# A transformer kernel whose modulation rows are summed by fused multiply-adds on VectorE

## The chip, the cores and the metric

The kernel runs as one program on 1 core of a Trainium2 chip. The time is the device time of one execution in microseconds. Before the change it was measured three times: 1494.89 us median, 1494.23 to 1496.46. The engines are TensorE (PE, with its weight loads as PEld), VectorE (DVE), ScalarE (ACT), GpSimd (POOL) and SyncE (SP), which here only issues transfers.

## The reference

Three transformer layers run one after the other on one sequence of 256 tokens of width 1024: a first block (sliding-window and differential attention, cross attention, an MLP of 4096) and two layers of a second block, each with two gated feed-forwards of 2816 and an attention part between them. All of it is float32. What the change touches is the modulation of the second block. Each of its two layers turns the vector `c` into nine rows of 1024 that shift, scale and gate the layer:

```
c_act = silu(c)                                   # 1024
for l in range(2):
    mod = c_act @ ada_w[l] + ada_b[l]             # 1024 x 9216 weights
    sh1, sc1, g1, sh2, sc2, g2, sh3, sc3, g3 = split(mod, 9)
    h = rms_norm(x, norm_g[l, 0]) * (1 + sc1) + sh1
    x = x + 0.5 * g1 * swiglu(h, ff_w13[l, 0], ff_w2[l, 0])
    h = rms_norm(x, norm_g[l, 1]) * (1 + sc2) + sh2
    x = x + g2 * (hybrid_conv_mla if l == 0 else nsa_attention)(h)
    h = rms_norm(x, norm_g[l, 2]) * (1 + sc3) + sh3
    x = x + 0.5 * g3 * swiglu(h, ff_w13[l, 1], ff_w2[l, 1])
```

The two modulation matrices are 75.5 MB of weights for a product with one vector.

## The kernel before, in words

**The weight stream.** All weights come from HBM in units of 128 x 2048 float32 (1 MB). `issue` (L383) puts their transfers on SP's queue in one fixed order, each into one of four `raw` buffers, as soon as a buffer is free. A matrix product in float32 accuracy is made of three: a unit is cut in two halves of 1024 columns, and of each half ACT makes a rounded part `whi` and DVE the remainder `wlo` (`pump`, L402, with the subtraction at L415). The activations are split in the same way (`hhi`/`hlo`, `gh`/`gl`, ...). TensorE then takes eight 128x128 tiles of a half and issues three matmuls of 256 columns for each, 24 a half. `pump` keeps the splits three halves ahead of TensorE.

**The order of the work.** The program is a list of steps (`Step`, L241). A step with weights is one half unit: pump, then what earlier steps have deferred, then its matmuls and, at the end of a pair of output tiles, the operations that take the result out of PSUM (`ft`, `x`, `q`, `k` and so on). Each engine takes its own instructions in the order in which the list emits them. In the feed-forwards and the MLP these steps follow each other; in the attention parts they are mixed with small steps of scores, softmax (`nm`, `p`, `r`), transposes (`pT`) and values (`o`).

**The modulation.** `ada_steps` (L716) cuts each matrix in nine sections of 1024 outputs and each section in four units `(s, q)` of two input blocks `k` of 128. A unit is a `raw` step: its 2048 columns are two rows of 1024 per partition, and `self.sc[:, k]` holds silu(c) for block `k`, one number per partition. The sum over the eight blocks is kept in a tile `adacc` of 128 x 1024. The unit is worked off in four pieces of 512 columns (`piece`). For `k == 0` ACT writes raw x sc into `adacc`. For the other seven blocks ACT scales the piece in place (`raw<-raw,sc`) and POOL adds it to `adacc` (L737). With the fourth piece the `raw` buffer is given back. When two sections are done, `rows` sums `adacc` over the partitions on TensorE (`ada<-adacc,Z`, eight matmuls of 512 columns), and `post` transposes the rows into the column tile `M` (`adat`), adding the bias on DVE.

`with_ada` (L783) spreads the 72 units over the steps from the 24th on to the 90th before the last that are not marked quiet. `ADA_LAGS` says how many such steps after the unit's place each of its parts is emitted: the four pieces 0, 0, 1 and 1 steps later, `rows` 3 and `post` 4 steps later.

Of the kernel before, what the change touches and what calls it, by code (L numbers as in the profile page):

```python
# [21 lines left out]
OP = mybir.AluOpType  # L22
# [4 lines left out]
D = 1024  # L27
# [8 lines left out]
LEAD = 1  # L36
HY = 14
NS = 20
ADA_DVE = ()
ADA_LAGS = (0, 0, 1, 1, 3, 4)  # L40
ADA_GAP = 2
GP = 64
NFILL = (0, 1, 4, 5, 10, 13)
# [249 lines left out]
class Kernel:  # L293
# [420 lines left out]
    def ada_steps(self, l):  # L714

        nc = self.nc  # L716
        st = {}
        steps = []
        M = self.M[l]

        def piece(s, q, n):
            kk, b = divmod(n, 2)
            k = 2 * q + kk

            def fn(raw):
                if k == 0 and b == 0:
                    st["acc", s] = self.w("adacc", [P, D], bufs=2)
                half = st["acc", s][:, b * 512:(b + 1) * 512]
                src = raw[:, n * 512:(n + 1) * 512]
                scale = self.sc[:, k:k + 1]  # L730
                if k == 0:
                    self.act(half, src, scale=scale)
                elif k in ADA_DVE:
                    nc.vector.scalar_tensor_tensor(half, src, scale, half, op0=OP.mult, op1=OP.add)
                else:
                    self.act(src, src, scale=scale)
                    nc.gpsimd.tensor_tensor(half, half, src, OP.add)  # L737
            return Step(fn, (f"ada{l}", 4 * s + q), raw=True, more=n < 3)

        def rows(r):  # L740
            def fn():
                ps = self.ps("ada", [P, 512], "T")
                for s in (2 * r, 2 * r + 1):
                    for jh in range(2) if s < 9 else ():
                        g = (2 * s + jh) % 4
                        self.mm(ps[32 * g:32 * g + 32, :], self.Z, st["acc", s][:, jh * 512:(jh + 1) * 512])
                n = P if r < 4 else 64
                st["sb"] = [self.t("adasb"), self.t("adasb")]
                for b in range(2):
                    self.act(st["sb"][b][:n], ps[:n, b * S:(b + 1) * S])  # L750
            return fn

        def post(r):
            def fn():
                M.have.update((2 * r, 2 * r + 1))
                n = P if r < 4 else 64
                sb = st["sb"]
                tp = self.ps("adat", [P, 4, P], "T")
                for c in range(4):
                    nc.tensor.transpose(tp[:, c, :n], sb[c // 2][:n, c % 2 * P:c % 2 * P + P], self.eye[:n, :n])  # L760
                for s in (2 * r, 2 * r + 1):
                    if s > 8:
                        continue
                    for jh in range(2):
                        g = (2 * s + jh) % 4
                        nc.vector.tensor_add(M[:, s, 4 * jh:4 * jh + 4], tp[:, :, 32 * g],
                                             self.ada_b[:, l, s, 4 * jh:4 * jh + 4])
                    if s in (1, 4, 7):
                        nc.vector.scalar_tensor_tensor(M[:, s, :], M[:, s, :], 1.0, self.norm_g[:, l, s // 3, :],
                                                       op0=OP.add, op1=OP.mult)  # L770
                    elif s in (2, 8):
                        nc.vector.tensor_scalar(M[:, s, :], M[:, s, :], 0.5, None, op0=OP.mult)
            return fn

        for s in range(9):
            for q in range(4):
                steps.append([piece(s, q, n) for n in range(4)])
            if s % 2 or s == 8:
                r = s // 2
                steps[-1] += [Step(rows(r)), Step(post(r))]  # L780
        return steps

    def with_ada(self, steps):  # L783
# [7 lines left out]
        for i in range(len(units)):  # L791
            at = lo + groups[i] * gap + i * (hi - lo - gap * groups[-1]) // len(units)
            for x, lag in zip(units[i], ADA_LAGS):
                where.setdefault(loud[at + lag], []).append(x)
# [1042 lines left out]
```

## Time and profile before

| | us |
|---|---|
| median of three runs | 1494.89 |
| the profiled execution | 1491.65 |
| its span on the core | 1489.9 |
| TensorE busy in it | 1437.3 |
| DVE / ACT / POOL busy | 1059.5 / 918.9 / 633.6 |

The span is what the trace covers, from the first instruction to the last. TensorE's granted clock is 0.995 of the full one over the run. Busy times of engines overlap, so a sum over engines means nothing; what counts is which engine a stretch waits for. A group of instructions is given by its line, engine, operation and `out<-in` by the names in the program, without buffer numbers.

### The profile page before, as it was taken

The numbers are of one execution on the slowest core, as the hardware profiler recorded it, in microseconds if no ns is written. First come the engines' busy times: TensorE is split into PE (matmuls) and PEld (weight loads), VectorE is DVE, ScalarE is ACT, GpSimd is POOL, SyncE is SP. The second block draws the span as 40 slices with busy tenths as digits, with TensorE's granted clock in tenths as the row PEclk, the third lists the DMA queues.
The fourth block names the chain that finished last, engine by engine and source line by source line (L and its number), as shares of the span: only waits on it lengthen the run. The fifth ranks groups of instructions, "written<-read, shape, count | busy, mean of one in ns | idle before, by whom it ended". The sixth has DMA issues, their size and how long they took to land.

```text
span 1489.9 us, 28338 instructions
## 1 busy us (share of the span) xinstructions
PE 1437.3 (96%) x11478; PEld 1374.9 (92%) x11478; DVE 1059.5 (71%) x1643; ACT 918.9 (62%) x1666; POOL 633.6 (43%) x466
## 2 busy tenths in 40 slices
PE   8998999999999999998899999999999999999997
PEld 8886989999989989998799999999999887999997
DVE  7877767776658777689887776677765788765553
ACT  6546767777657567664667666676654665644442
POOL 3002433545874566753356658546453200500021
PEclk9999999999999999999999999999999999999998
DMA  8344646777665777754447877568773620355451
GB/s 319 116 142 170 218 151 227 244 270 273 260 246 199 278 267 272 257 186 170 169 171 272 295 262 296 206 238 300 259 278 132 219 80 25 118 198 196 173 182 45
DMA packets 46067, 312.00 MB, mean 209 GB/s; under 512 B 5232, under 2 KB 7024, under 8 KB 9072
## 3 DMA queue, kind: packets, MB, share of 16 engines
q1 hardware_dynamic: 45936, 310.19, 57.8%
q8 instruction: 90, 1.47, 0.4%
q14 instruction: 41, 0.34, 0.1%
HBM read 309.12 MB, written 1.05 MB: 208 GB/s over the span
## 4 chain that ended last, share of the span: by engine, by line
PE 64%; DVE 16%; ACT 8%; DMA 7%; issue 2%; POOL 1%; SPq 0%; POOLq 0%; ACTq 0%; DVEq 0%
PE mm L356 57%; DVE wlo L415 6%; DMA raw<-w 4%; ACT whi L329 2%; ACT raw L329 2%; PE sc L356 2%; PE o L356 1%; DVE p L849 1%; POOL adacc L737 1%; PE mmt L356 1%; DVE hlo L664 1%; DMA raw<-w_up 1%; DMA raw<-w_down 1%; DVE gl L353 1%; ACT p L329 1%
## 5 line engine op out<-in xcount | busy, mean ns | idle before, releaser
L415 DVE TENSOR_TENSOR wlo<-raw,whi 128x1024 fp32r<-128x1024 f32 (+2 forms) x438 | 627.2, 1438 | 52.2 <-ACT whi L329 51.7
L737 POOL TENSOR_TENSOR adacc<-adacc,raw 128x512 f32<-128x512 f32 x252 | 430.8, 1734 | 415.8 <-ACT raw L329 331.4
L356 PE MATMUL mm<-hlo,whi 128*128 128x256 f32 x1960 | 556.6, 284 | 6.0 <-DVE hlo L664 4.1
L356 PE MATMUL mm<-hhi,whi 128*128 128x256 f32 (+1 forms) x1960 | 558.0, 285 | 1.5 <-ACT whi L329 1.5
L356 PE MATMUL mm<-hhi,wlo 128*128 128x256 f32 (+1 forms) x1960 | 553.3, 282 | 5.2 <-DVE wlo L415 5.2
L329 ACT ACTIVATE whi<-raw 128x1024 fp32r<-128x1024 f32 (+2 forms) x438 | 453.2, 1044 | 110.6 <-DMA raw<-w 72.5
L356 PEld LDWEIGHTS mm<-hlo,whi 128*128 128x128 f32 x1960 | 369.9, 189 | 9.6 <-DVE hlo L664 5.6
L356 PEld LDWEIGHTS mm<-hhi,wlo 128*128 128x128 f32 x1960 | 371.2, 189 | 7.3 <-DVE wlo L415 7.0
L356 PEld LDWEIGHTS mm<-hhi,whi 128*128 128x128 f32 x1960 | 370.2, 189 | 5.4 <-DVE wlo L415 1.7
L356 PE MATMUL mm<-gh,whi 128*128 128x256 f32 x960 | 272.6, 284 | 0.0
L356 PE MATMUL mm<-gh,wlo 128*128 128x256 f32 x960 | 271.6, 283 | 0.0
L356 PE MATMUL mm<-gl,whi 128*128 128x256 f32 x960 | 271.6, 283 | 0.0
L356 PEld LDWEIGHTS mm<-gh,whi 128*128 128x128 f32 x960 | 184.2, 192 | 4.3 <-issue 3.4
L356 PEld LDWEIGHTS mm<-gl,whi 128*128 128x128 f32 x960 | 184.2, 192 | 0.0
L356 PEld LDWEIGHTS mm<-gh,wlo 128*128 128x128 f32 x960 | 184.2, 192 | 0.0
L329 ACT ACTIVATE raw<-raw,sc 128x512 f32<-128x512 f32 x252 | 167.0, 712 | 0.6 <-DMA raw<-ada 0.5
L1410 DVE TENSOR_TENSOR ft<-mm,ft 128x256 f32<-128x256 f32 x79 | 33.4, 423 | 110.0 <-ACT ft L329 109.8
L353 DVE TENSOR_TENSOR gl<-ft,gh 128x256 fp32r<-128x256 f32 x120 | 74.0, 628 | 46.2 <-ACT gh L329 46.0
L580 POOL TENSOR_SCALAR xg<-x,M 128x256 f32<-128x256 f32 x40 | 55.9, 1398 | 97.4 <-DVE x L1273 91.2
L329 ACT ACTIVATE p<-sc,nm 128x128 f32<-128x128 f32 (+1 forms) x120 | 49.8, 420 | 66.5 <-DVE r L840 18.7
L329 ACT ACTIVATE ft<-mm 128x256 f32<-128x256 f32 x79 | 29.9, 379 | 96.3 <-PE mm L356 96.1
L596 POOL TENSOR_TENSOR acc<-acc,sq 128x256 f32<-128x256 f32 x60 | 60.8, 1016 | 43.5 <-ACT sq L329 37.0
(298 smaller groups left out, 1878.6 us busy)
## 6 DMA issues: line engine op xcount, KB each, us to landing
raw<-w SPq DMA_DIRECT2D x132, 1024.0 KB, 4.9
raw<-ada SPq DMA_DIRECT2D x72, 1024.0 KB, 6.4
raw<-w_up SPq DMA_DIRECT2D x16, 1024.0 KB, 5.0
raw<-w_down SPq DMA_DIRECT2D x16, 1024.0 KB, 5.2
raw<-hy_in SPq DMA_DIRECT2D x8, 1024.0 KB, 5.2
raw<-w_in SPq DMA_DIRECT2D x6, 1024.0 KB, 7.8
raw<-nsa_in SPq DMA_DIRECT2D x6, 1024.0 KB, 5.0
raw<-w_ck SPq DMA_DIRECT2D x4, 1024.0 KB, 4.9
```

The costliest lines, as they stand in the source:

```text
L329: return self.nc.scalar.activation(out, in_, func, **k)
L353: self.nc.vector.tensor_tensor(lo, src, hi.bitcast(F), OP.subtract)
L356: self.nc.tensor.matmul(out, lhsT, rhs, start=start, stop=stop, skip_group_check=True)
L415: self.behind = lambda hi=hi[:, :b - a], lo=lo[:, :b - a], src=src: self.nc.vector.tensor_tensor(lo, src, hi.bitcast(F), OP.subtract)
L580: nc.gpsimd.tensor_scalar(st["xg", c], xc, gain(c), None, op0=OP.mult)
L596: nc.gpsimd.tensor_tensor(acc, st["acc" + key], sq, OP.add)
L664: nc.vector.scalar_tensor_tensor(*last, op0=OP.add, op1=OP.subtract)
L737: nc.gpsimd.tensor_tensor(half, half, src, OP.add)
L849: nc.vector.tensor_scalar(p[n], p[n], r[:, n:n + 1], None, op0=OP.mult)
L1410: nc.vector.tensor_mul(s, ps[:, 1, :], s)
```

## The change

The sum over the blocks moves to DVE. A unit is now worked off in two pieces of 1024 columns, one for each of its blocks. For `k == 0` ACT still writes the scaled piece into `adacc`, in one operation instead of two. For the other blocks one `scalar_tensor_tensor` on DVE computes adacc = raw x sc + adacc (L732 of the new file). ACT no longer scales in place, and POOL no longer adds. The two pieces are emitted 0 and 1 steps after the unit's place, `rows` and `post` 3 and 4 steps, as before.

```
--- before.py
+++ after.py
@@ -36,8 +36,7 @@
 LEAD = 1
 HY = 14
 NS = 20
-ADA_DVE = ()
-ADA_LAGS = (0, 0, 1, 1, 3, 4)
+ADA_LAGS = (0, 1, 3, 4)
 ADA_GAP = 2
 GP = 64
 NFILL = (0, 1, 4, 5, 10, 13)
@@ -719,23 +718,19 @@
         M = self.M[l]
 
         def piece(s, q, n):
-            kk, b = divmod(n, 2)
-            k = 2 * q + kk
+            k = 2 * q + n
 
             def fn(raw):
-                if k == 0 and b == 0:
+                if k == 0:
                     st["acc", s] = self.w("adacc", [P, D], bufs=2)
-                half = st["acc", s][:, b * 512:(b + 1) * 512]
-                src = raw[:, n * 512:(n + 1) * 512]
+                acc = st["acc", s]
+                src = raw[:, n * D:(n + 1) * D]
                 scale = self.sc[:, k:k + 1]
                 if k == 0:
-                    self.act(half, src, scale=scale)
-                elif k in ADA_DVE:
-                    nc.vector.scalar_tensor_tensor(half, src, scale, half, op0=OP.mult, op1=OP.add)
+                    self.act(acc, src, scale=scale)
                 else:
-                    self.act(src, src, scale=scale)
-                    nc.gpsimd.tensor_tensor(half, half, src, OP.add)
-            return Step(fn, (f"ada{l}", 4 * s + q), raw=True, more=n < 3)
+                    nc.vector.scalar_tensor_tensor(acc, src, scale, acc, op0=OP.mult, op1=OP.add)
+            return Step(fn, (f"ada{l}", 4 * s + q), raw=True, more=n < 1)
 
         def rows(r):
             def fn():
@@ -774,7 +769,7 @@
 
         for s in range(9):
             for q in range(4):
-                steps.append([piece(s, q, n) for n in range(4)])
+                steps.append([piece(s, q, n) for n in range(2)])
             if s % 2 or s == 8:
                 r = s // 2
                 steps[-1] += [Step(rows(r)), Step(post(r))]
```

The orders of TensorE and of the transfer queue are the same as before. What moves stands on DVE, ACT and POOL. The names: `wlo<-raw,whi` is the remainder of a weight half, `ft` the result of a pair of output tiles, `gl` the remainder of the squared result, `adacc` the modulation's sum.

DVE before, towards the end of the MLP's up projection (around 340 us):

```order
L415 TENSOR_TENSOR wlo<-raw,whi 128x1024
L353 TENSOR_TENSOR gl<-ft,gh 128x256 x2
L415 TENSOR_TENSOR wlo<-raw,whi 128x1024
L1356 SCALAR_TENSOR_TENSOR ft<-mm,rbs 128x256 x2
L415 TENSOR_TENSOR wlo<-raw,whi 128x1024
L353 TENSOR_TENSOR gl<-ft,gh 128x256 x2
```

And now at the same place:

```order
L414 TENSOR_TENSOR wlo<-raw,whi 128x1024
L352 TENSOR_TENSOR gl<-ft,gh 128x256 x2
L732 SCALAR_TENSOR_TENSOR adacc<-raw,sc,adacc 128x1024
L414 TENSOR_TENSOR wlo<-raw,whi 128x1024
L1351 SCALAR_TENSOR_TENSOR ft<-mm,rbs 128x256 x2
L732 SCALAR_TENSOR_TENSOR adacc<-raw,sc,adacc 128x1024
L414 TENSOR_TENSOR wlo<-raw,whi 128x1024
L352 TENSOR_TENSOR gl<-ft,gh 128x256 x2
```

A fused operation stands ahead of the remainder of the next step's weights; it comes behind the deferred `gl` and behind the `ft` of the step that it follows.

ACT before, a little earlier in the same phase (`gh` is the rounded part of the squared result, `sc` the column of silu(c)):

```order
L329 ACTIVATE whi<-raw 128x1024
L329 ACTIVATE gh<-ft 128x256 x2
L329 ACTIVATE raw<-raw,sc 128x512 x2
L329 ACTIVATE whi<-raw 128x1024
L329 ACTIVATE ft<-ft 128x256 x2
L329 ACTIVATE raw<-raw,sc 128x512 x2
L329 ACTIVATE whi<-raw 128x1024
```

And now:

```order
L328 ACTIVATE whi<-raw 128x1024
L328 ACTIVATE gh<-ft 128x256 x2
L328 ACTIVATE whi<-raw 128x1024
L328 ACTIVATE ft<-ft 128x256 x2
L328 ACTIVATE whi<-raw 128x1024
```

The scalings between the rounded parts of the weights are gone.

DVE before, in the hybrid block's attention (around 700 us; `k`, `v`, `nm`, `r` and `p` are its keys, values, row maxima, reciprocal sums and probabilities):

```order
L1514 TENSOR_TENSOR k<-mm,rbs 64x256 x8
L415 TENSOR_TENSOR wlo<-raw,whi 128x1024
L347 TENSOR_SCALAR v<-mm,rr 128x256 x2
L817 TENSOR_REDUCE nm<-sc 128x1
L818 TENSOR_REDUCE nm<-sc 128x1
L415 TENSOR_TENSOR wlo<-raw,whi 128x1024
L817 TENSOR_REDUCE nm<-sc 128x1
L818 TENSOR_REDUCE nm<-sc 128x1
L840 RECIPROCAL r<-sm 128x2
```

And now:

```order
L1509 TENSOR_TENSOR k<-mm,rbs 64x256 x8
L414 TENSOR_TENSOR wlo<-raw,whi 128x1024
L346 TENSOR_SCALAR v<-mm,rr 128x256 x2
L732 SCALAR_TENSOR_TENSOR adacc<-raw,sc,adacc 128x1024
L812 TENSOR_REDUCE nm<-sc 128x1
L813 TENSOR_REDUCE nm<-sc 128x1
L414 TENSOR_TENSOR wlo<-raw,whi 128x1024
L732 SCALAR_TENSOR_TENSOR adacc<-raw,sc,adacc 128x1024
L812 TENSOR_REDUCE nm<-sc 128x1
L813 TENSOR_REDUCE nm<-sc 128x1
L835 RECIPROCAL r<-sm 128x2
```

Two fused operations now stand ahead of the row maxima of a head.

## Rows read from the trace of the kernel before

**Rows 1.** The page: busy us, share and instructions of each engine.

```profile
PE 1437.3 (96%) x11478; PEld 1374.9 (92%) x11478; DVE 1059.5 (71%) x1643; ACT 918.9 (62%) x1666; POOL 633.6 (43%) x466
```

**Rows 2.** Stretches: busy us (x) of PE, PEld, DVE, ACT, POOL; clock, DMA, GB/s.

```profile
111.00:260.00 149.00, 141.91 (x1009) 129.31 (x1008) 110.07 (x208) 101.39 (x211) 52.81 (x40) 1.00 0.54 191
260.00:345.00 85.00, 82.52 (x674) 79.84 (x674) 63.68 (x85) 63.75 (x116) 42.86 (x28) 1.00 0.73 253
345.00:666.00 321.00, 315.56 (x2579) 307.43 (x2579) 231.01 (x256) 209.61 (x333) 209.61 (x134) 1.00 0.69 250
685.00:737.00 52.00, 40.98 (x289) 34.77 (x287) 48.29 (x94) 27.43 (x65) 16.43 (x12) 0.97 0.53 189
777.00:1110.00 333.00, 331.29 (x2738) 325.04 (x2738) 235.52 (x256) 226.29 (x352) 201.79 (x123) 1.00 0.73 267
1304.00:1474.00 170.00, 169.46 (x1417) 169.33 (x1416) 91.42 (x118) 74.83 (x109) 12.25 (x9) 1.00 0.48 168
```

**Rows 3.** Waits of weight loads, 260:1110 us: total, times, longest.

```profile
PEld ada L356 <- POOL adacc L737: 9.7, 9, 2.1
PEld mm L356 <- DVE wlo L415: 6.1, 8, 2.1
```

**Rows 4.** Waits of matmuls, whole run.

```profile
PE ada L356 <- POOL adacc L737: 3.8, 4, 1.2
```

**Rows 5.** The chain of waits: start us, us, what.

```profile
320.05 4.82 DMA raw<-w_up
...
337.39 1.23 ACT raw L329 x2
339.58 2.70 POOL adacc L737 x2
...
346.87 43.21 PE mm L356 x360
```

**Rows 6.** Groups, whole run: busy us, mean ns | idle before.

```profile
L415 DVE TENSOR_TENSOR wlo<-raw,whi 128x1024 fp32r<-128x1024 f32 x431 | 622.0, 1449 | 51.6 <-ACT whi L329 51.3
L353 DVE TENSOR_TENSOR gl<-ft,gh 128x256 fp32r<-128x256 f32 x120 | 74.0, 628 | 46.2 <-ACT gh L329 46.0
...
L574 DVE SCALAR_TENSOR_TENSOR hml<-mem,colp,hmh 128x256 fp32r<-128x256 f32 x8 | 3.6, 476 | 0.0
...
L737 POOL TENSOR_TENSOR adacc<-adacc,raw 128x512 f32<-128x512 f32 x252 | 430.8, 1734 | 415.8 <-ACT raw L329 331.4 <-issue 81.7 <-POOL adacc L737 1.5
...
L329 ACT ACTIVATE raw<-raw,sc 128x512 f32<-128x512 f32 x252 | 167.0, 712 | 0.6 <-DMA raw<-ada 0.5
```

**Rows 7.** Groups on DVE, 1332:1406 us, POOL silent.

```profile
L415 DVE TENSOR_TENSOR wlo<-raw,whi 128x1024 fp32r<-128x1024 f32 x27 | 32.8, 1216 | 0.0
...
L353 DVE TENSOR_TENSOR gl<-ft,gh 128x256 fp32r<-128x256 f32 x13 | 5.4, 416 | 0.0
```

**Rows 8.** Waits of the transfer queue for a buffer, whole run.

```profile
SPq L394 <- POOL adacc L737: 333.5, 72, 8.8
```

**Rows 9.** Groups on DVE, 685:737 us.

```profile
L415 DVE TENSOR_TENSOR wlo<-raw,whi 128x1024 fp32r<-128x1024 f32 x8 | 12.2, 1531 | 0.0
L849 DVE TENSOR_SCALAR p<-p,r 128x256 f32<-128x256 f32 x8 | 6.9, 866 | 0.0
...
L849 DVE TENSOR_SCALAR p<-p,r 128x128 f32<-128x128 f32 x8 | 3.9, 488 | 0.3
```

**Rows 10.** Groups on DVE, 1221:1258 us, POOL nearly silent.

```profile
L849 DVE TENSOR_SCALAR p<-p,r 128x256 f32<-128x256 f32 x16 | 5.8, 365 | 0.0
L849 DVE TENSOR_SCALAR p<-p,r 128x128 f32<-128x128 f32 x16 | 4.8, 302 | 0.6
```

**Rows 11.** Order of time on DVE, 682:710 us: start, us, instructions.

```profile
685.41 3.59 DVE L886 TENSOR_TENSOR q<-rt,rt 32x256 f32<-32x256 f32 x4
...
689.82 1.71 DVE L886 TENSOR_TENSOR q<-rt,rt 32x256 f32<-32x256 f32 x4
```

**Rows 12.** Groups on DVE, 111:260 us.

```profile
L574 DVE SCALAR_TENSOR_TENSOR hlo<-x,colp,hhi 128x256 fp32r<-128x256 f32 x16 | 13.3, 851 | 2.3 <-ACT hhi L329 2.3
```

## The prediction

> **What bounds the kernel now.** I read the page's table of engines first. TensorE is busy 96% of the span, VectorE (DVE) 71%, ScalarE (ACT) 62%, GpSimd (POOL) 43% [rows 1]. Busy time of pipelined matmuls is modelled, so I went on to the windows and counted matmuls. From 1304 to 1474 us, where no modulation work is left, TensorE issues 1417 in 170 us, 120.0 ns each. In the feed-forward stretches with modulation work, 345 to 666 and 777 to 1110, it is 124.5 and 121.6 ns, and 126.1 ns from 260 to 345 [rows 2]. At 120.0 ns those three would take 80.9 + 309.5 + 328.6 = 719 us and not 739: all that can be won there is 20 us, the modulation's own 512-wide matmuls and the norm transitions included. The kernel is bound by TensorE there, and only TensorE's stalls count.
>
> The waits of its weight loads name them: from 260 to 1110 us, 9 waits of 9.7 us together for POOL's `adacc`, and 8 of 6.1 us for `wlo` [rows 3]. The matmuls' own waits show 3.8 us for `adacc` [rows 4], since a matmul still in the pipeline covers part of a stalled load. The chain of waits shows how such a stall comes about: ACT scales two halves of `raw` (1.23 us), POOL adds them (2.70 us, up to 342.3), and then TensorE runs 43.21 us on matmuls alone [rows 5]. So the stall at 342 was POOL being late, not weights running out.
>
> The other kind of place is 685 to 737 us, the latency-bound attention of the hybrid block: DVE busy 48.3 of 52 us, and TensorE issues only 289 matmuls [rows 2]. There every DVE microsecond is nearly one of the program.
>
> **The change, part by part.** Removed: 252 ACT scalings of 128x512 (167.0 us) and 252 POOL additions (430.8 us) [rows 6]. Added: 126 fused operations of 128x1024 on DVE (18 sections of 8 blocks, the first block of each staying on ACT, now as one operation instead of two). The rows show no fused operation of that size, so I build it: with POOL silent, a tensor-tensor takes 1216 ns for 1024 and 416 for 256 columns [rows 7], which is 1.04 ns a column; a fused one from SBUF takes 476 ns for 256 [rows 6]; 476 + 768 x 1.04 = 1.28 us. Bounds: 1.22 us (no dearer than the tensor-tensor) and, if the fused one paid double per column, 2.1 us; I take 1.28, since its 256-wide row lies 60 ns above the tensor-tensor's. 126 x 1.28 = 161 us more for DVE.
>
> DVE also gets time back. `wlo` takes 1449 ns over the whole run against 1216 where POOL is silent, and `gl` 628 against 416 [rows 6, 7]: 431 x 0.233 + 120 x 0.212 = 126 us lengthening beside POOL. Of POOL's 633.6 us the additions are 430.8, 68%, so about 85 us go. DVE ends near 1059.5 + 161 - 85 = 1135 us, 76%, ACT near 750, POOL near 200. None of this is on the path yet; the path takes five terms.
>
> 1. The waits for `adacc`. The order of TensorE and of the DMA queue is unchanged. The last fused operation of a row pair is two steps ahead of the row's matmuls. On DVE it stands right behind a `wlo` that TensorE needs before 24 matmuls (2.9 us), so its 1.28 us, even with two `gl` of 0.42 ahead, end in their shadow. The 9.7 us go; the bounds are 3.8 (the matmul side) and 9.7. I take -7: each of nine loads hides part of its stall under running matmuls.
>
> 2. The waits for `wlo`, 6.1 us. In these stretches a weight unit lands, ACT splits it, DVE splits it, and only then does its buffer take the next transfer. Out of that loop go ACT's 1.23 us and DVE's lengthening; in comes 1.28 us. The modulation units, too, give back their buffer when POOL has added: the DMA queue waited 333.5 us for that, 72 times [rows 8], 4.6 us each. Bounds 0 and -6.1; I take -2, near zero, because DVE's gain and cost nearly cancel.
>
> 3. From 685 to 737 us. Six fused operations enter DVE's order there: +7.7. Given back: `wlo` 8 x (1531 - 1216), `p` 8 x (866 - 365) and 8 x (488 - 302) [rows 7, 9, 10] = 2.5 + 4.0 + 1.5, and the four `q` of 3.59 us that take 1.71 when POOL is silent [rows 11], 1.9: together 9.9. POOL's 12 instructions in that stretch [rows 2] are the 12 additions that the six replace, so all of it goes. Net -2.2, I take -2; bounds +7.7 (nothing given back) and -9.9 (the fused ones in gaps).
>
> 4. From 111 to 260 us, attention with DVE at 110 of 149 us [rows 2]: 14 fused operations, +17.9, against 16 `hlo` at 851 ns, where the same operation on `hml` took 476 [rows 12, 6], -6.0, and smaller pieces; ACT's pairs of scalings (1.23 us [rows 5]) leave the same chains. Upper bound (17.9 - 6.0) x 0.74 = +8.8; lower -4, three such pairs out of the chain. I take 0.
>
> 5. New DVE work in the feed-forward stretches. The tightest is the up projection before 345 us: per pair of output tiles DVE has 2 `wlo` and 4 operations of 256 columns, 2 x 1.216 + 4 x 0.416 = 4.10 us, plus 14 fused ones in 13 pairs, 1.38: 5.48 against 48 matmuls of 120 ns, 5.76. DVE's idle time hides it, 0.28 us a pair. If the cover is gone (fused at 2.1 us: 6.36) it costs 13 x 0.6 = 8. I take +1; bounds 0 and +8. Queued behind a fused operation on DVE is the `wlo` of the next step, with three splits of lead. The transfer it waits for precedes its weights in the queue: ACT waited 0.5 us for it in all 252 scalings [rows 6].
>
> On term 5 the Trainium skill has something to say against the change: SBUF — State Buffer, "Who interferes with whom", has a DVE instruction with two SBUF inputs contend with GpSimd instructions that read SBUF, and a fused operation has two. The `hlo` at 851 against 476 ns shows it [rows 12, 6]. By that rule some 14% of the 126 (POOL's remaining 200 us of 1490) are lengthened by 0.4 us, 7 us of DVE busy time, off the path; without it, none; the sum is the same within 1 us.
>
> Sum: -7 - 2 - 2 + 0 + 1 = -10 us. The profiled execution took 1491.65 us (span 1489.9), so 1481.65; it lies 3.24 below the median of 1494.89, so the forecast for the median is 1484.9, **1485 us**, 0.7% less.
>
> **Rivals.** (a) Hidden anyway: the stall at the row matmuls only gave the splits a lead, and without it TensorE meets a late `wlo` instead. For it: the chain before 342 us runs through transfers and ACT. Against it: 43 us of pure matmuls follow at once [rows 5]. With 7 of the 9 us of terms 1 and 2 given back the sum is -3, 1492, with all of them -1, 1494; I price it at 1493.
>
> (b) Slower: DVE becomes the pacer of the two attention stretches. For it: 48.3 of 52 and 110 of 149 us busy [rows 2], in chains in which each operation waits for the one before. The 20 fused operations cost, by those shares, 6 x 1.28 x 0.93 + 14 x 1.28 x 0.74 = 20.4 us; if half of what I count as given back (9.9 + 6.0) comes, 8, that is +12.4, less 7 of term 1: +5.4, 1500. It decides as soon as less than 13 us comes back there. Against it: POOL is otherwise silent there. The Trainium skill's Perfetto Trace Analysis, "Optimizing Scalar/DVE Operations", advises to move work to ScalarE or GpSimd where DVE is saturated, the reverse of this change; its own addition, that GpSimd and DVE share a read port, is what speaks for my sum.
>
> (c) That the change doesn't do what it says is excluded by the order: 126 fused operations, none on POOL.
>
> **How the numbers follow.** Forecast 0.62 (1478 to 1491), (a) 0.20, (b) 0.18. Faster or slower than 1494.89 by over 0.2% (3 us) is what a measurement tells from no change. Faster: 0.62 x 0.95 + 0.20 x 0.25 = 0.64; slower: 0.18 x 0.9 = 0.16; the rest, 0.20, within. The range reaches from 1477, where term 3 or 2 comes out full, to 1498, which takes in (a) and the better half of (b).
>
> **What would show it.** Right: no wait of TensorE for the accumulator; `wlo` near 1.25 us; the fused operation near 1.28; 685 to 737 shorter by some 2 us; DVE near 1135 busy. Wrong: the fused operation above 1.6 us; new waits for `wlo` as long as those removed; a longer stretch from 111 to 260 us; `wlo` still above 1.4 us, which would mean that POOL was not what lengthened it.

## The result, and the profile after

Four runs of the changed kernel have a median of 1473.02 us (1472.16 to 1473.70), four of the kernel before 1495.20 (1494.23 to 1496.46): the ratio is 0.9851, 95% interval 0.9834 to 0.9868. The change is 22 us faster; 10 were forecast, and the time lies under the stated range. The profiled execution after took 1473.70 us (span 1471.9), 18 us less than the profiled one before.

The page of the kernel after, the engine line that answers to [rows 1]:

```profile
PE 1431.7 (97%) x11478; PEld 1377.2 (94%) x11478; DVE 1074.9 (73%) x1769; ACT 763.9 (52%) x1396; POOL 214.0 (15%) x214
```

ACT and POOL came out near the forecast (750 and 200). DVE is 60 us under the forecast 1135: it took on 163.5 us and still grew by only 15. The groups on DVE over the whole run, to be held against [rows 6]:

```profile
L414 DVE TENSOR_TENSOR wlo<-raw,whi 128x1024 fp32r<-128x1024 f32 x431 | 534.5, 1246 | 10.8 <-ACT whi L328 10.4
L732 DVE SCALAR_TENSOR_TENSOR adacc<-raw,sc,adacc 128x1024 f32<-128x1024 f32 x126 | 163.5, 1298 | 0.4 <-ACT adacc L328 0.4
L352 DVE TENSOR_TENSOR gl<-ft,gh 128x256 fp32r<-128x256 f32 x120 | 51.7, 441 | 9.8 <-ACT gh L328 9.6
```

The fused operation takes 1298 ns (1.28 us was estimated), `wlo` 1246 (1.25). Of the 126 us that `wlo` and `gl` were lengthened beside POOL, 87.5 and 22.3 came back, 87% and not two thirds; the rest of the 148 us came from smaller operations.

The stretches of the program that answer to [rows 2], in the same columns, from 109.5, 258.3, 338.5, 672.5 and 762.8 us on:

```profile
109.50:258.30 148.80, 143.14 (x1021) 130.87 (x1021) 116.91 (x223) 85.08 (x183) 13.43 (x12) 1.00 0.54 191
258.30:338.50 80.20, 80.20 (x672) 79.22 (x671) 68.45 (x99) 47.92 (x87) 0.00 (x0) 1.00 0.76 278
338.50:651.00 312.50, 310.49 (x2576) 306.47 (x2576) 230.50 (x296) 157.06 (x240) 57.94 (x50) 1.00 0.69 255
672.50:722.80 50.30, 42.52 (x288) 36.78 (x287) 44.83 (x100) 21.35 (x56) 0.00 (x0) 0.90 0.53 190
762.80:1092.50 329.70, 329.15 (x2736) 324.49 (x2736) 242.72 (x304) 164.69 (x246) 33.90 (x25) 1.00 0.75 270
```

In the up projection before 338.5 us POOL is silent, and TensorE issues a matmul every 119.3 ns, where it was 126.1: at the rate of the free stretch, though DVE is busy 85% of it. The waits of weight loads that answer to [rows 3], over the whole run, hold no `adacc`, and of `wlo` only what lies ahead of 258.3 us, outside those stretches:

```profile
PEld mm L355 <- DVE wlo L414: 2.8, 3, 1.2
```

The chain of waits that answers to [rows 5] has nothing but TensorE in this part:

```profile
299.90 36.22 PE mm L355 x303
336.11 0.99 PE ada L355 x8
337.11 3.06 PE mm L355 x24
```

**Where the time went.** TensorE issues the same 11,478 matmuls in the same order in both traces, so their starts can be compared one by one. This table gives how much longer each stretch takes than in the kernel after, in microseconds (shorter where it is negative); the edges are times in the trace of before. The modulation's own matmuls, which some experiments move, are left out of the matching. The kernels other than before are those of the next section.

```
                111-260  260-685  685-777  777-1110   whole run
before             +1.7    +11.4     +1.7      +3.1       +18.1
before_again       +1.7    +11.8     +1.8      +5.1       +20.7
after_again        -0.0     +0.0     -0.0      -0.0        -0.5
rows_late          +0.2     +5.5     +1.5      +1.4        +8.9
narrow_dve         +0.9     -0.0     +0.8      -0.0        +1.5
act_ghost          +0.2     -1.5     -0.1      -0.1        -1.5
act_scales        +12.5     +6.1     +6.1      +2.3       +27.3
wide_old           +7.5    +16.6     +2.4      +9.5       +35.4
pool_paced         +2.9     +0.0     +1.4      +0.0        +4.4
pool_paced5        +8.4    +25.7     +3.4     +12.7       +50.1
pool_release1      +0.3     +4.9     +0.1      -0.0        +4.5
pool_release2      +2.3    +11.9     +0.9      +6.1       +21.0
pool_release       +7.4    +39.4     +2.0     +27.9       +76.0
pool_raw          +13.5    +42.8     +4.8     +32.0       +93.5
no_fused           -4.0     -1.5     -6.2      -0.0       -11.6
hy_quiet           +0.0     -0.0     -6.0      +1.5        -5.1
late54_quiet       -5.9     +0.1     -4.8      +1.5        -7.3
```

Within the stretches the 18.1 us of before sit in few places. At six of its ten row steps, where TensorE sums a pair of modulation rows (340, 424, 547, 597, 941 and 1099 us) TensorE loses 1.8, 3.2, 2.8, 0.1, 2.8 and 0.4 us, 10.9 together (from six matmuls before the row's to thirty behind); at the places of the waits for `wlo` (319, 331 and 527 to 542 us, and smaller ones) 5.1; in the attention before 260 us 1.7, in the hybrid block 1.7. Against it stand 1.5 us at 650 us, where the granted clock of the kernel after falls to half.

### The profile page after: what moved, and what is told of

Its sections match the earlier page's. It is cut to its first block, busy times and chain, and to the rows that moved or that the text cites. A ratio compares the mean times of both kernels' runs of the same rounds, so it can differ in the third digit from the quotient of the medians.

```text
span 1471.9 us, 27739 instructions
## 1 busy us (share of the span) xinstructions
PE 1431.7 (97%) x11478; PEld 1377.2 (94%) x11478; DVE 1074.9 (73%) x1769; ACT 763.9 (52%) x1396; POOL 214.0 (15%) x214
## 4 chain that ended last, share of the span: by engine, by line
PE 80%; DVE 14%; ACT 3%; issue 2%; DMA 1%; POOL 0%; SPq 0%; POOLq 0%; ACTq 0%; DVEq 0%
PE mm L355 73%; DVE wlo L414 3%; PE sc L355 2%; PE o L355 2%; PE mmt L355 1%; DVE hlo L663 1%; DVE adacc L732 1%; ACT p L328 1%; DVE p L844 1%; PE ada L355 1%; PE pT L851 1%; DVE nm L813 1%; PE ssum L355 1%; DVE hlo L573 1%; DMA raw<-nsa_in 0%
## 5 line engine op out<-in xcount | busy, mean ns | idle before, releaser
L414 DVE TENSOR_TENSOR wlo<-raw,whi 128x1024 fp32r<-128x1024 f32 (+2 forms) x438 | 539.7, 1238 | 11.3 <-ACT whi L328 10.7
L328 ACT ACTIVATE whi<-raw 128x1024 fp32r<-128x1024 f32 (+2 forms) x438 | 451.7, 1045 | 120.4 <-DMA raw<-w 70.9
L732 DVE SCALAR_TENSOR_TENSOR adacc<-raw,sc,adacc 128x1024 f32<-128x1024 f32 x126 | 163.5, 1298 | 0.4 <-ACT adacc L328 0.4
L579 POOL TENSOR_SCALAR xg<-x,M 128x256 f32<-128x256 f32 x40 | 62.6, 1566 | 575.5 <-DVE x L1268 569.2
L1268 DVE SCALAR_TENSOR_TENSOR x<-mm,M,x 128x256 f32<-128x256 f32 x48 | 23.2, 483 | 81.4 <-PE mm L355 81.3
L328 ACT ACTIVATE hhi<-x,M 128x256 fp32r<-128x256 f32 x40 | 20.4, 511 | 91.7 <-DVE x L1268 91.7
```

What stands on the lines that cost most here:

```text
L328: return self.nc.scalar.activation(out, in_, func, **k)
L414: self.behind = lambda hi=hi[:, :b - a], lo=lo[:, :b - a], src=src: self.nc.vector.tensor_tensor(lo, src, hi.bitcast(F), OP.subtract)
L579: nc.gpsimd.tensor_scalar(st["xg", c], xc, gain(c), None, op0=OP.mult)
L732: nc.vector.scalar_tensor_tensor(acc, src, scale, acc, op0=OP.mult, op1=OP.add)
L1268: nc.vector.scalar_tensor_tensor(xc, ps, gate(m), xc, op0=OP.mult, op1=OP.add)
```

## The experiments

**Only the row steps.** The lags of `rows` and `post` in the kernel before:

```
-ADA_LAGS = (0, 0, 1, 1, 3, 4)
+ADA_LAGS = (0, 0, 1, 1, 5, 6)
```

> The kernel before, with the rows of the modulation summed two steps later (lags 5 and 6 instead of 3 and 4); nothing moves to another engine. Theory: matched by their number, TensorE's matmuls lose 10.9 us at the ten row steps of before; with two more steps POOL is done when they come, so 10 to 11 us go: 1484 us (1481 to 1487), and no wait for adacc is left. Rival (hidden anyway): the stall only lets the splits catch up, and without it TensorE waits for wlo instead: 1490 to 1495.

It took 1482.08 us (1481.11 to 1482.95), before on the same chip 1493.32 (ratio 0.9929, 0.9911 to 0.9947), and the changed kernel, run again beside it, 1472.97 (0.9871, 0.9847 to 0.9895). So 11.2 us go with two numbers and no work moved. The waits of weight loads for `wlo` in the whole run of before, and then the rows of this run that name `wlo` or `adacc`:

```profile
PEld mm L356 <- DVE wlo L415: 8.6, 11, 2.1
```

```profile
PEld mm L356 <- DVE wlo L415: 5.7, 13, 1.0
...
PEld sc L356 <- POOL adacc L737: 0.3, 1, 0.3
```

No row matmul waits for `adacc`, and the waits for `wlo` did not grow in its place. Rival (a), hidden anyway, falls here. The expectation for the yardstick:

> The changed kernel once more, as the yardstick for the others on the same chip. 1473 us, 22 us under before (bounds 1471 to 1475). What is open is whether the 18 us between the two profiled executions or the 22 us between the medians is the size of the change.

Its trace lies within 0.5 us of the first at every stretch. A second trace of before was taken too:

> The kernel before once more, for a second trace. Its times so far go from 1488.5 to 1496.5 us, while the changed kernel stays within 1472 to 1475.5 and the one with late rows within 1481 to 1483. If the spread of before lies in its waits for adacc, the stages against the first trace differ at the row steps; if it lies in attention or in the half clock, there.

It is 2.6 us longer than the first: 1.7 at row steps, most of the rest at waits for `wlo` that came and went (-1.3 at 319 us; +1.5 at 494 to 500 and +0.7 at 1045); in the attention and behind 1110 us the two agree within 0.3. Over all runs before ranged from 1488.5 to 1496.5 us, the changed kernel from 1471.9 to 1475.5. With its first profile (1491.65 us) the kernel before had drawn an execution below all four of the result: between the profiles the gain is 18 us, between the medians of the two sets in which both ran 22.2 and 20.3.

**The width and the engines.** The kernel before has a switch for fused operations on DVE, in its four pieces of 512 columns:

```
-ADA_DVE = ()
+ADA_DVE = tuple(range(1, 8))
```

> The kernel before with its four pieces of 512 columns and its lags, every block but the first fused on DVE: 252 fused operations of 512 instead of 126 of 1024, 36 writes on ACT instead of 18. Theory: the engine and the fusing decide; the 126 more instructions cost DVE some 0.06 us each, 8 us of busy time that is off the path: 1474 (1472 to 1478). Rival (the width is worth something): 1480 or more.

1474.97 us (1474.43 to 1475.16; 0.9896 of before, 0.9880 to 0.9912); the fused operation takes 758 ns, 180.7 us in all, 17 more than after. The width is worth about 2 us; the trace has it in the two attention stretches (0.9 and 0.8).

Then the wide pieces with the old engines, and with the addition alone moved:

```
 wide_old and act_scales, in place of the fused operation:
+    self.act(src, src, scale=scale)
 wide_old:
+    nc.gpsimd.tensor_tensor(acc, acc, src, OP.add)
 act_scales:
+    nc.vector.tensor_tensor(acc, acc, src, OP.add)
```

> The changed kernel's two pieces of 1024 and its lags, but scaled by ACT and added by POOL as before. Theory: the engine decides and not the width; the additions take as long in all, so the time is that of before, 1495 us (1490 to 1500), with the waits for adacc still there. Rival (fewer, wider operations are what helped): 1480 us.

> The changed kernel, but ACT still scales each piece of 1024 in place and DVE only adds it: POOL is silent as after the change, ACT is loaded as before. Theory: POOL's lateness and the lengthening of DVE beside it are what cost, so nearly all of the gain stays: 1475 us (1473 to 1479). Rival (the waits for wlo came from ACT, whose scalings stand ahead of whi): the 5.2 us of those waits stay, 1479 to 1483.

Both expectations were wrong. `wide_old` took 1508.99 us (1505.53 to 1509.70; ratio 1.0105, 1.0084 to 1.0126), `act_scales` 1500.64 (1498.05 to 1501.45; 1.0049, 1.0033 to 1.0066), slower than before although POOL adds nothing in it. In `wide_old` the weight loads wait 19.2 us for `wlo` and still 7.3 for `adacc`. The waits of DVE in `act_scales` point to why:

```profile
DVE adacc L733 <- ACT raw L328: 99.7, 92, 3.4
```

92 of 126 additions reach the head of DVE's queue before ACT has scaled, 1.1 us each time, and the `wlo`, the row maxima and the evictions queued behind them wait too: weight loads wait 8.4 us for `wlo`, where it was 2.8, and 6.2 us for `x`, the result of a pair of output tiles. In the kernel before the same wait stood on POOL (331.4 us [rows 6]), where more than half of the instructions were these additions (252 of 466). In the changed kernel it is 0.4 us. So the fusing is what makes the move to DVE pay: without it the move costs 27 us more. Not all of the 27 us are DVE's waits: TensorE's granted clock is 0.986 over this run and 0.992 over the changed kernel's, which is worth up to 9 us (an estimate from these two figures and the spans, 1499.3 and 1471.9 us).

**ACT's load alone.** The changed kernel, with scalings beside the fused operation that nobody reads:

```
+    for i in range(3):
+        self.act(self.ghost, src[:, i * 204:(i + 1) * 204], scale=scale)
```

> The changed kernel, and beside each fused operation three scalings of 204 columns of the same piece on ACT into a scratch tile that nobody reads: ACT is loaded about as before, POOL stays silent, DVE waits for none of it. Theory A (the waits for wlo came from ACT's scalings ahead of whi): the 5.2 us of wlo waits and part of the attention's 1.7 come back, 5 to 7 us over the changed kernel, 1479. Theory B (they came from DVE lengthened beside POOL): 0 to 2 over, 1474.

1473.53 us (1472.30 to 1474.01; 0.9885, 0.9869 to 0.9902). The groups on ACT:

```profile
L328 ACT ACTIVATE ghost<-raw,sc 128x204 f32<-128x204 f32 x378 | 174.8, 462 | 8.2
```

That is more than the 167.0 us removed [rows 6], and it costs nothing. So ACT's load by itself was not what the change gained. This run does not put back the order of before, in which POOL waited for the scalings; their 1.23 us in the chain before 342 us [rows 5] were a step of that chain.

**The fused work alone.** Each fused operation cut to one column, which leaves nearly all of the sum out:

```
-    nc.vector.scalar_tensor_tensor(acc, src, scale, acc, op0=OP.mult, op1=OP.add)
+    nc.vector.scalar_tensor_tensor(acc[:, :1], src[:, :1], scale, acc[:, :1], op0=OP.mult, op1=OP.add)
```

> The changed kernel with each fused operation cut to one column, so that waits and buffers stay and 126 x 1.2 us = 151 us of DVE's work go (the sum over the modulation's blocks is left out). It prices the work that the change puts on DVE. Theory: nothing in the feed-forwards (its waits for wlo are 2.8 us in the whole run), and in the two attention stretches less than the 20 fused operations last, 4 to 8 us: 1467 (1464 to 1471). Rival (DVE's share of 73% makes it a pacer): 10 us or more, under 1463.

1462.62 us (1462.19 to 1463.62; 0.9814 of before, 0.9798 to 0.9831), 10.4 below the changed kernel. In the table all of it lies in the attention before 260 us (4.0) and in the hybrid block (6.2), apart from the 1.5 us of the clock at 650. The 106 fused operations in the feed-forwards cost nothing. The expected range was missed, and the time is that of its rival, but not for the rival's reason: DVE does not pace the whole run, the 20 fused operations in the two attention stretches cost more than was thought. The half clock is not what they cost in the hybrid block: its granted clock is 0.90 there in the changed kernel, and `act_ghost`, with the same fused operations, was granted 0.97 and took the same time within 0.1 us.

**POOL's reading, and its late giving back.** These kernels put POOL's work back into the changed kernel and differ in who waits for it; of each edit the lines that count:

```
 pool_ghost, beside each fused operation (lasthi: the newest whi):
+    for i in range(self.lasthi.shape[-1] // 204):   # 5 for 1024 columns
+        nc.gpsimd.tensor_tensor(self.ghost, self.ghost, self.lasthi[:, i * 204:(i + 1) * 204], OP.add)
 pool_paced (pool_paced5: range(5)):
     ...                                             # at: one column of a small tile
+    self.act(at, src[:, 0:1])                       # one column
+    nc.gpsimd.tensor_tensor(self.ghost[:, 0:1], self.ghost[:, 1:2], at, OP.mult)
+    for i in range(3):
+        nc.gpsimd.tensor_tensor(self.ghost, self.ghost, self.ghost, OP.add)
 pool_release (1 and 2: range(1), range(2)), in the loop of pool_paced:
+        nc.gpsimd.tensor_tensor(self.ghost, self.ghost, src[:, i * 204:(i + 1) * 204], OP.add)
 pool_raw, for the two halves of src:
+    nc.gpsimd.tensor_tensor(half, half, half, OP.add)
```

> The changed kernel, and beside each fused operation five additions of 204 columns on POOL, of the newest rounded weights to a scratch tile that nobody reads: POOL reads and adds about as much as before, and nobody waits for its sums (five buffers' worth of steps pass before the rounded weights are overwritten). Theory B: wlo goes back to some 1.45 us on average, the 5.2 us of wlo waits come back and the two attention stretches lose up to 8 us more, 5 to 13 over the changed kernel, 1482. Theory A: DVE is lengthened but has room for it outside the attention, 1 to 5 over, 1476.

1554.98 us (1551.93 to 1556.04; 1.0428, 1.0404 to 1.0452), and it tells nothing of the reading: POOL was busy 685.3 us with these additions, and ACT waited 132.9 us for it before it could write the next rounded weights. That wait was not meant to be there. Hence `pool_paced`:

> The changed kernel, and beside each fused operation one column and three additions of 204 columns on POOL, of a scratch tile to itself, started by a one-column write of ACT: some 410 us of POOL as in before (431), and neither ACT nor DVE nor a buffer waits for it (in pool_ghost ACT waited 132.9 us for POOL to be done with the rounded weights, which spoiled it). Theory B (DVE is lengthened beside POOL, and that was the rest of the gain): wlo back to 1.40 to 1.45 us, 5 to 10 us over the changed kernel, 1480, the loss in the up projections where the waits for wlo were and in the two attention stretches. Theory L (POOL's reading costs nothing, only its late release of buffers and its late sums did): within 2 us of the changed kernel, 1474.

1478.16 us (1477.78 to 1481.55; 0.9913, 0.9893 to 0.9933). Its groups on DVE and POOL:

```profile
L414 DVE TENSOR_TENSOR wlo<-raw,whi 128x1024 fp32r<-128x1024 f32 x431 | 571.7, 1332 | 9.3 <-ACT whi L328 8.9
L732 DVE SCALAR_TENSOR_TENSOR adacc<-raw,sc,adacc 128x1024 f32<-128x1024 f32 x126 | 175.0, 1389 | 0.4 <-ACT adacc L328 0.4
```

```profile
L738 POOL TENSOR_TENSOR ghost<-ghost 128x204 f32<-128x204 f32 x378 | 379.5, 1004 | 29.6
```

DVE is lengthened, by 42% of what `wlo` was in before, and loses 2.9 and 1.4 us in the attention stretches. In the feed-forwards the table has 0.0, but this trace lacks the half clock at 650 us that the kernel after has (granted clock 1.00 from 260 to 685 us), so that 1.5 us are lost there too, 1.1 of them between 500 and 540 us, where before waits for `wlo`. So the time lies between the two expectations. The full dose failed:

> As pool_paced with five additions instead of three beside each fused operation: some 650 us of POOL, wlo at about the 1.45 us of before, no buffer and no engine waiting. If the full lengthening of DVE made the waits for wlo: 3 to 6 us more than pool_paced in the stretches from 260 to 666 us, 1485 or more. If not: the feed-forwards stay as in the changed kernel and only the two attention stretches grow, 1480 to 1483.

1523.91 us (1523.11 to 1524.73; 1.0211, 1.0190 to 1.0231). `wlo` rose only to 1364 ns (58% of the lengthening of before), while POOL, now busy 869.7 us, was late with its own sums for the norms. The waits of weight loads in it:

```profile
PEld ssum L355 <- POOL acc L595: 22.5, 4, 10.5
...
PEld mm L355 <- DVE wlo L414: 5.0, 8, 1.2
```

What the lengthening of before costs in full stays open, though at 1364 ns the waits for `wlo` are 2.2 us more than after. Then the giving back of the transfer buffer:

> As pool_paced, but the three additions read the modulation piece itself, so that its raw buffer is given back only when POOL is done, some 3.6 us after ACT's start, as before. If the late release made the waits for wlo: about 5 us of them come back between 260 and 666 us, 1483. If not: pool_paced's 1478.

> The changed kernel, and after each fused operation POOL adds the piece to itself in place, twice 512 columns as before: the buffer is given back late, DVE is lengthened in full, nobody needs the result. If the late release and the lengthening together made the waits for wlo: 4 to 7 us in the feed-forwards and 4 to 8 in the attention stretches, 1484. If neither does, the feed-forwards stay and it is 1478 to 1480, and what is left is the scaling on ACT that POOL waited for.

1548.83 us (1547.16 to 1555.55; 1.0386, 1.0357 to 1.0414) and 1565.97 (1561.86 to 1567.14; 1.0487, 1.0465 to 1.0509): the expected 5 us were 67 and 75 in the feed-forwards (the second and fourth stretch of the table). To see where before stands on that slope, I counted how many of TensorE's matmuls have started when the last reader of each of the 72 modulation units is done, and took the difference from the kernel after, at 0.12 us a matmul. This measures when a unit's buffer is given back against TensorE's progress. On average a unit is given back 3.9 us later in before, 0.6 in `pool_paced`, 5.1 in `pool_release`, 5.2 in `pool_raw`. Two smaller doses followed:

> As pool_release with one addition on POOL instead of three beside each fused operation. The buffer should come free some 2 us later than in the changed kernel, half of what it was in before. If the late release made the waits for wlo, with an edge near the 3.9 us of before: 0 to 2 us in the feed-forwards, 1475 (1473 to 1477). If each microsecond of lateness costs alike: 67 x 2 / 5.1 = 26 us there, 1500.

> As pool_release with two additions instead of three. The buffer should come free some 3.5 to 4 us later, as in before. If the late release made the waits for wlo of before: 3 to 15 us in the feed-forwards and 2 to 4 in the attention stretches, 1483 (1478 to 1490). If lateness costs alike all along: 67 x 3.7 / 5.1 = 49 us, 1524.

The first took 1475.47 us (1474.97 to 1477.95; 0.9887, 0.9872 to 0.9901) and gives a unit back 1.3 us later by that count; the second took 1497.04 (1493.63 to 1499.64; 1.0031, 1.0014 to 1.0048), 3.6 us later, more than was expected. Weight loads waited for `wlo`, with one, two and three additions on POOL:

```profile
PEld mm L355 <- DVE wlo L414: 5.8, 6, 2.1
```

```profile
PEld mm L355 <- DVE wlo L414: 16.7, 16, 4.0
```

```profile
PEld mm L355 <- DVE wlo L414: 38.1, 31, 4.1
```

ACT's wait for the transfers of weights does not rank the kernels in this way. It is 70.9 us after; before, in `pool_paced`, and with one, two and three additions it is:

```profile
ACT whi L329 <- DMA raw<-w: 72.5, 36, 5.3
```

```profile
ACT whi L328 <- DMA raw<-w: 94.8, 43, 4.4
```

```profile
ACT whi L328 <- DMA raw<-w: 91.3, 41, 4.6
```

```profile
ACT whi L328 <- DMA raw<-w: 146.1, 57, 5.2
```

```profile
ACT whi L328 <- DMA raw<-w: 200.5, 54, 9.2
```

So before shows hardly more of it than after, and `pool_paced`, which loses 1.5 us in the feed-forwards, more than `pool_release1`, which loses 4.9.

`pool_release2` lengthens `wlo` no more than `pool_paced` (1325 against 1332 ns) and loses 18.0 us in the feed-forwards where that lost 1.5: between these two it is the late buffer and not the longer `wlo`. `pool_release1` loses 4.9 us there, of which 3.6 are one wait of 2.1 us at 390 us and the half clock that came behind it; its profiled execution is also the slowest of its four, by 2.4 us. The loss grows faster than the delay (4.9, 18.0 and 67.3 us of the feed-forwards for 1.3, 3.6 and 5.1 us), in part through the clock: in these two stretches, 453 and 358 us long in `pool_release`, TensorE's granted clock was 0.974 and 0.976, after the change 0.996 and 1.00, which is worth up to 19 of the 67 us (an estimate from these figures).

Before gives back as late as `pool_release2` and loses much less, 5.1 us at the waits for `wlo`; that DVE carries no fused work in it may be why. And its own chain of waits does not run through POOL's buffers at the places of the waits for `wlo`. From 285 to 335 and from 495 to 535 us it has seven transfers; six of them wait for a buffer that `wlo` gives back, none for one of POOL's. Of the first and the second stretch (the transfer at 320.05 us behind the first row is in [rows 5]):

```profile
317.76 2.23 DVE wlo L415
```

```profile
532.15 2.24 DVE wlo L415
...
534.44 5.42 DMA raw<-w
```

Such a `wlo` takes 2.2 us where an undisturbed one takes 1.22 [rows 7], `pool_paced` lost 1.5 us with 42% of the lengthening, and no run lengthens `wlo` as much as before does. So the runs show that a late buffer can cost this kernel much; they do not show that it made the 5.1 us. No run takes only the late giving back, or only the lengthening, out of the kernel before.

**A better version.** The hybrid block's steps marked quiet, so that no unit is placed there; and, on top, the first unit later:

```
+        for s in zr + uq + ukv + outs[:2]:
+            s.quiet = True
 late54_quiet also:
-ADA_FROM = 24
+ADA_FROM = 54
```

> The changed kernel with the hybrid block's steps marked quiet, so that the modulation units that stood there (six fused operations) go to the steps around it. From the run without fused operations: the hybrid stretch cost 6 to 7.9 us more with them (685 to 737, and the half clock at 650 that came with it); in the feed-forwards they cost nothing. So 1466 (1464 to 1470). Rival (the cost comes back as a later modulation row or as transfers that collide): 1471 to 1475.

> As hy_quiet, and the first unit placed 54 steps into the list instead of 24, so that most of the fused operations leave the cross attention before 260 us too, where the run without them was 3.3 to 4 us shorter. 1463 to 1465 if nothing else binds; 1468 to 1475 if the 72 transfers of 1 MB, now in a shorter time, make the weights late before 345 us.

1469.84 us (1468.66 to 1472.38; 0.9858, 0.9835 to 0.9881) and 1466.64 (1465.66 to 1467.55; 0.9831, 0.9813 to 0.9848). The first lies in its expected range, the second between its two expectations. The two stretches give what the run without fused work promised (6.0; then 5.9 and 4.8). Each loses 1.5 us again between 777 and 1110 us, and the second 1.6 behind it. The waits for `wlo` are unchanged (2.7 and 2.8 us). `late54_quiet` is the fastest kernel that computes the whole reference, some 25 us under before.

## Why the prediction fell short

The direction was right, and so were the lengths of the single operations (`wlo`, the fused one, `p`). Terms 1, 2 and 4 were mis-sized, and term 5 was counted for a cost that never came. Between the two profiles they make -3.9, -3.1, -1.7 and -1 of the 8 us by which these lie further apart than forecast, against 1.5 us of half clock.

- **Term 1, the waits for `adacc`** (-7 of at most 9.7): measured -10.9, by place and by `rows_late`. The step that failed is that "each of nine loads hides part of its stall under running matmuls". It hides none: at 424 us the loads waited 2.9 us and TensorE lost 3.2, at 547 and 941 us 2.5 and 2.8 each. The matmuls' own waits [rows 4] were the wrong bound. That TensorE lost even some 0.3 us more than the waits at each of these places is not explained by a run.
- **Term 2, the waits for `wlo`** (-2 of at most 6.1): measured -5.1. The loop was named rightly. The step that failed is that "DVE's gain and cost nearly cancel": the fused work costs nothing in the feed-forwards (`no_fused`), so there was nothing to set against the gain. What the gain consists of stays open. ACT's load is worth nothing by itself (`act_ghost`). Left are DVE's lengthening, through which the chain of before runs, and the modulation unit's own buffer, which goes back 3.9 us sooner by TensorE's matmuls. That row was there [rows 8] and its 333.5 us were quoted, and then left out of the sum.
- **Term 3, the hybrid block** (-2): measured -1.7. Six fused operations cost 6.2 us (7.7 counted), and 7.9 came back (9.9 counted), so that the sum is near in part because two errors offset each other. In its groups between 672 and 723 us `wlo`, the fused operation and both `p` run at their undisturbed lengths, as was reckoned from [rows 9 to 11]:

```profile
L414 DVE TENSOR_TENSOR wlo<-raw,whi 128x1024 fp32r<-128x1024 f32 x8 | 9.7, 1218 | 0.0
L732 DVE SCALAR_TENSOR_TENSOR adacc<-raw,sc,adacc 128x1024 f32<-128x1024 f32 x6 | 7.7, 1279 | 0.0
...
L844 DVE TENSOR_SCALAR p<-p,r 128x256 f32<-128x256 f32 x8 | 2.8, 348 | 0.0
L844 DVE TENSOR_SCALAR p<-p,r 128x128 f32<-128x128 f32 x8 | 2.3, 287 | 0.3
```

- **Term 4, attention from 111 to 260 us** (0, between -4 and +8.8): measured -1.7. The 14 fused operations cost 4.0 us and not 13: most of their 17.9 us were hidden, so DVE's busy share of 74% was no price for an inserted operation. And 5.7 us came back, about the 6.0 counted.
- **Term 5, new work in the feed-forwards** (+1): 0, by `no_fused`. That 5.48 us of DVE fit into the 5.76 of a pair was right; the +1 had no measured cause.
- **Rival (b)**, DVE as the pacer, is half true: the fused operations do cost 10.2 us in the two stretches, but 13.6 came back there (7.9 and 5.7), just above the 13 at which it would have decided.
- **The scale.** The 3.24 us between the profiled execution and the median of before were carried over unchanged. The second trace of before is longer than the first mostly at its waits for `adacc` and `wlo`, which the change removes; so the 4 us by which the medians lie further apart than the profiles, of the 12 missed, probably belong to them too. The timed runs have no trace that would show it.

On the rule of the Trainium skill in SBUF — State Buffer, "Who interferes with whom": the runs agree that a DVE operation with two SBUF inputs is lengthened beside POOL's reads (fused 1279 ns with POOL silent, 1389 in `pool_paced`), and the whole run lost 126 x (1298 - 1279) = 2.4 us of DVE to it, off the path.

## What to carry to other kernels

Here a stalled weight load of a full TensorE was lost time one for one (9.7 us of waits, 10.9 lost); take the sum of such waits as the gain, not the matmuls' part of it. When an operation changes its engine, look at what stands behind its wait in the new queue: ACT's scaling handed to DVE instead of POOL made the kernel 27 us slower than the fused operation did, and fusing the hand-over away is what made this move pay. Of a streaming kernel, ask of every change when it gives back a transfer buffer, measured against the consumer's progress: between 3.6 and 5.1 us of delay the loss rose from 18 to 67 us. And look whom the chain of waits names before calling a cause found: a mechanism that costs much when it is put in need not be the one that was taken out.

## What was not expected of the hardware

On POOL a product of one column takes 585 ns and an addition of 204 columns 1004 (`pool_paced`), where an addition of 512 columns took 1734 [rows 6]: 4.9 ns a column against 3.4, so that an addition cut into pieces keeps POOL busier. And the granted clock of TensorE fell to half, 1.2 of 2.4 GHz, for a few microseconds at 650 us after the change, not in before and not in `act_ghost`, although TensorE had done nearly the same in the 5 us ahead in the two kernels. First the changed kernel, then `act_ghost`, both from 645 us in steps of 5; the clock is the third number from the end:

```profile
645.00:650.00 5.00, 4.26 (x35) 4.18 (x36) 4.02 (x11) 2.12 (x6) 0.00 (x0) 1.00 0.61 210
650.00:655.00 5.00, 5.00 (x31) 5.00 (x31) 3.81 (x7) 4.60 (x7) 0.00 (x0) 0.66 0.31 105
```

```profile
645.00:650.00 5.00, 4.25 (x35) 4.16 (x35) 4.02 (x11) 2.10 (x6) 0.00 (x0) 1.00 0.63 210
650.00:655.00 5.00, 5.00 (x43) 5.00 (x43) 3.81 (x7) 4.62 (x7) 0.00 (x0) 1.00 0.28 105
```

TensorE does 12 matmuls fewer in the second row, which is the 1.5 us of the table. What decides whether the clock falls there stays open.
